# Moving the first weight pairs of the mLSTM merge behind the attention projection's last split, and its form loads behind the weight loads

## The chip, the cores and the metric

One core of a Trainium2 chip runs the whole program. The metric is the time of one execution on the device in microseconds (us), given as the median of several runs; lower is better. Beside the runs there is one profiled execution, whose trace is read below. Engine names are those of the profile: PE (TensorE matmuls), PEld (its weight loads), DVE (VectorE), ACT (ScalarE), POOL (GpSimd), SP (SyncE, which only issues DMAs here).

## The reference

One step of a hybrid decoder layer on 512 prompt tokens and 8 x 4 sample tokens, 544 columns in all, width 2048. An input projection feeds an mLSTM branch and a sliding-window attention branch. What matters here is the end of it:

```
y = (sigmoid(g_m) * einsum('btc,cd->btd', br_m, w_proj_m)
     + sigmoid(g_a) * einsum('btc,cd->btd', br_a, w_proj_a))
out = einsum('btc,cd->btd', y, w_out)
return _layernorm(DN_ALPHA * x + out, ln_w, ln_b)
```

The three matrices are 2048 x 2048, all data float32.

## The kernel before

Every large product is split into high and low parts. A weight block of 128 columns is loaded in two halves of 8 x 128 rows ("raw", 512 KB each, `load_half`, L205). `split` makes `wh` on ACT (a cast, L212) and then `wl = raw - wh` on DVE (L213). PE multiplies wh by the high and the low activation and wl by the high one. There are three buffers for raw halves loaded by L205, two for each of wh and wl, and so a split for the next product waits on PE releasing the one before the last.

Three stages meet at the place of the change.

1. **The attention projection** (`wa_`, 16 column blocks, `ct` 0 to 15, in `gemm`, matmuls at L229). Each block takes two halves; its two PSUM banks are multiplied into a tile `c5` on DVE (L1559) and stored (`d_t`, L1560).
2. Beside the last blocks, `first_forms` reads quarters of the mLSTM branch (`d_brm`, L1445), makes the forms f11, f1, f2, f12 (high and low) and stores two more forms to DRAM (`d_n3` at L1469, `d_s4` at L1479). The tiles for this come from a pool `fr` of four buffers.
3. **The merge** (`paired`, eight pairs of blocks of `w_proj_m`, matmuls at L634 for wh and L636 for wl). A pair is a seven-product scheme of the Strassen kind: seven half products, called steps 0 to 6 here, each 24 matmuls, instead of eight. Their weights are b11, b12 (raw, L205), b21, b22 (raw2, L605) and sums: step 1 takes `t1 = b11 + b12` and step 2 `b11 = t1 + b22`, both DVE additions at L614; two more sums are accumulating DMAs issued by POOL (L612). `prepare` emits the sums and the split up to two steps ahead, with a raised priority. The activations of the steps are the forms f11, f1, f2, f12, f3, f4, f22 in this order.

The first call of the generator `beside_merge` reads f3 back from `d_n3` (four DMAs into `fr`, `chunks_of`, `fetched`), then f4 from `d_s4` (four more, which wait for the f3 tiles to be free) and f22 into `room` (one 1088 KB DMA, L1501), and splits them (ACT L1492, DVE L1493). Steps 4, 5 and 6 need them. Gathering of the banks is done by `gather` (L644 to L663).

After the merge the output product begins in `first_two` (L1729), which splits four halves of `w_out`; just ahead of it the last columns of y are cast (`hilo`, ACT L265, DVE L266).

The order of instructions on each engine is worked out when the program is built, by a list scheduler with priorities: `tc.high_priority(offset=...)` raises what is emitted in it, `behind(...)` (`tc.issue_after`) keeps what is emitted in it behind a named earlier instruction in that order; neither adds a wait on the chip. PE's order in the merge is that of the code (`manual_schedule`). On the chip each of ACT, DVE, POOL and SP then takes its instructions in this order.

Of the kernel before, what the change touches and what calls it, by code (L numbers as in the profile page):

```python
# [5 lines left out]

# [1 line left out]

# [1 line left out]

# [68 lines left out]
def _build(tc, nc, i, o, es):  # L81
# [41 lines left out]
    def nm(s):  # L123
        count[0] += 1
        return f"{s}_{count[0]}"
# [7 lines left out]
    def r32(ap):  # L133
        return ap.bitcast(F32)
# [13 lines left out]
    state = {}  # L148
# [53 lines left out]

    def load_half(wv, c0, half):
        raw = wr.tile([128, 8, 128], F32, tag="raw", name=nm("raw"))
        state["load"] = nc.sync.dma_start(raw[:], wv[:, half * 8:half * 8 + 8, c0:c0 + 128])  # L205
        return raw

    def split(raw, p=None, tags=("wh", "wl")):
        p = p or wp
        wh = p.tile([128, 8, 128], F32R, tag=tags[0], name=nm("wh"))  # L210
        wl = p.tile([128, 8, 128], F32R, tag=tags[1], name=nm("wl"))
        state["wh"] = A.copy(wh[:], raw[:])  # L212
        state["wl"] = V.tensor_tensor(out=wl[:], in0=raw[:], in1=r32(wh[:]), op=ALU.subtract)  # L213
        return wh, wl

    @contextmanager
    def behind(*what):

        with ExitStack() as st:
            for w in what:  # L220
                st.enter_context(tc.issue_after(state[w].ins))
            yield
# [376 lines left out]
    def load_a(w):  # L599
        w["b11"], w["b12"] = (load_half(w["wv"], c0, 0) for c0 in (w["cA"], w["cB"]))  # L600

    def load_b(w):
        for n, c0 in (("b22", w["cB"]), ("b21", w["cA"])):
            w[n] = raw2()
            state["load"] = nc.sync.dma_start(w[n][:], w["wv"][:, 8:16, c0:c0 + 128])  # L605

    def prepare(w, n):


        def add(out, a, b):  # L610
            if w.get("acc") and out == a and n != 2:
                G.dma_start(out=w[out][:], in_=w[b][:], accum_op=ALU.add)  # L612
            else:
                V.tensor_tensor(out=w[out][:], in0=w[a][:], in1=w[b][:], op=ALU.add)  # L614
        if n == 1:
            w["t1"] = raw2()
            add("t1", "b11", "b12")
        elif n == 2:
            add("b11", "t1", "b22")
        w["hl", n] = split(w[("b11", "t1", "b11", "b21", "b12", "b22", "b21")[n]])  # L620
        if n == (1 if w.get("acc") else 3):
            add("b12", "b12", "b22")
        elif n == (3 if w.get("acc") else 4):
            add("b21", "b21", "b11")
# [40 lines left out]
    AHEAD = 400  # L665

    def paired(work, first=iter(()), early=False):

        steps = [(w, n) for w in work for n in range(7)]
        ready = 0  # L670
        load_a(work[0])
        load_b(work[0])
        for at, (w, n) in enumerate(steps):

            while ready < min(at + 3, len(steps)):
                with tc.high_priority(offset=AHEAD):
                    prepare(*steps[ready])
                ready += 1
            if early and at == 0:
                next(first)  # L680
            p = at // 7 + 1
            if n == 4 and "fetch" in w:
                w["fetch"]()
            if p < len(work):
                if n == 3:
                    load_a(work[p])
                elif n == 4:
                    load_b(work[p])
            half_product(w, n)
            with tc.high_priority(offset=AHEAD):  # L690
                gather(w, n)
            next(first, None)
            if n == 6:
                w["end"](w["O1"], w["O2"])
            tick()
# [741 lines left out]
    def fr():  # L1437
        return late["fr"].tile([128, 2, HT], F32, tag="fr", name=nm("fr"))

    def fetched(srcs, own=None):  # L1440
        out = []
        with behind("load"):
            for src in srcs:
                st = fr() if out or own is None else own
                nc.sync.dma_start(st[:], src.rearrange("k p t -> p k t"))  # L1445
                out.append(st[:] if st is not own else own)
        return out
# [47 lines left out]
    def beside_merge(f3, f4, f22, room):  # L1495

        split_form(f3, chunks_of(d_n3), -1.0)
        raws = chunks_of(d_s4)
        stage = room[0][:].rearrange("p a (b t) -> p (a b) t", b=2)
        with behind("load"):  # L1500
            nc.sync.dma_start(stage, d_brm[8:16, :, HT:T].rearrange("k p t -> p k t"))  # L1501
        yield
        yield
        split_form(f4, raws)
        for n in range(4):
            if n < 3:
                yield
            split_form(f22, [stage[:, n * 2:n * 2 + 2]], at=n)
        for _ in range(44):
            yield  # L1510

        def ask(ct, eng):
            late[ct] = c5t()[:]
            eng.dma_start(late[ct], d_y[ct])

        for ct in range(2):
            ask(ct, nc.sync)
        yield
        for ct in range(0, 14, 2):
            if ct % 4 == 0:  # L1520
                yh_.append(act3.tile([128, 4, T], F32R, tag="act", name=nm("yh")))
                yl_.append(act3.tile([128, 4, T], F32R, tag="act", name=nm("yl")))
            with behind("wh", "wl"):
                for c in (ct, ct + 1):
                    hilo(late[c], yh_[-1][:, c % 4], yl_[-1][:, c % 4])
                    if c < 4:
                        ask(c + 2, nc.gpsimd)
            yield
# [48 lines left out]
    wo_raw = [load_half(wo, 0, 0), load_half(wo, 128, 0), load_half(wo, 0, 1)]  # L1577
# [135 lines left out]
    def first_two():  # L1713

        both = [mm(True), mm(True)]
        for half in range(2):
            ws = []
            for ct in range(2):
                ws.append(split(wo_raw[half * 2 + ct]))
                if half == 0 and ct == 1:  # L1720
                    wo_raw.append(load_half(wo, 128, 1))
                    load_rows(0)
            for k0 in (0, 4):
                for ps, (wh, wl) in zip(both, ws):
                    for kk in range(k0, k0 + 4):
                        k = half * 8 + kk
                        for n, (a, b) in enumerate(((wh, yh), (wh, yl), (wl, yh))):
                            for f, c, w in CUT:
                                PE.matmul(ps[ALL, f, 0:w], a[:, kk], b(k, c, w),  # L1729
                                          start=(k == 0 and n == 0), stop=(k == 15 and n == 2))  # L1730
        return both
# [19 lines left out]
    for g in range(G3):  # L1751
        ct = 16 - G3 + g
        ps = sm()
        for half in range(2):
            raw = load_half(wo, ct * 128, half)
            if g < 2:
                wh, wl = (w[:, :, g] for w in w2[half])
                hilo(raw[:], wh, wl)
            else:
                w1.append(split(raw))  # L1760
                wh, wl = w1[half]
# [41 lines left out]
```

## Time and profile before

| | |
|---|---|
| median of 3 runs | 2522.78 us (2520.69 to 2524.19) |
| the profiled execution's own time | 2525.29 us |
| its span, first to last instruction | 2523.5 us |
| mean granted TensorE clock | 0.993 |
| PE busy / PEld busy | 2479.2 us (98%) / 2416.3 us (96%) |
| DVE / ACT / POOL busy | 1779.1 (71%) / 1212.5 (48%) / 366.8 (15%) us |
| attention projection's last half, start of merge, end of merge | 2114.6, 2130.7, 2300.3 us from the span's start |

How to read the rows below: the timeline gives start and duration of an instruction (or of equal ones that follow each other, xcount) and in square brackets the idle time of its engine just before it and what ended that. The table by stretches gives, for each stretch, its length and for each engine its busy time and number of instructions, then the mean granted clock (PEclk), the DMA engines' busy share and GB/s. The chain is the work that ended last, followed back from the program's end.

### The profile page before, as it was taken

The page shows a single profiled execution, that of the slowest core. Times are in us where ns is not written, and L with a number is a line of the kernel's source. Part 1 is how long each engine was busy: PE and PEld are TensorE (multiplying, and loading weights), DVE is VectorE, ACT ScalarE, POOL GpSimd, SP SyncE. Part 2 cuts the span into 40 slices and gives each one's busy share as a digit, 9 for nine tenths or more (in the row PEclk, how much of TensorE's full clock was granted, in tenths as well). Part 3 has the DMA queues.
Part 4 walks back from the last instruction along what each step waited for, and adds up shares of the span by engine and source line. Part 5 has one row for each costly group of instructions (what it writes and reads, how often), then busy time and mean ns, then how long its engine had stood idle before and what let it go on. Part 6 is the DMA issues. An engine that isn't in the chain of part 4 may idle for free.

```text
span 2523.5 us, 48930 instructions
## 1 busy us (share of the span) xinstructions
PE 2479.2 (98%) x19803; PEld 2416.3 (96%) x19803; DVE 1779.1 (71%) x2614; ACT 1212.5 (48%) x1971; POOL 366.8 (15%) x442
## 2 busy tenths in 40 slices
PE   8999999999999999999999999999999998999997
PEld 7999999999999999998999999999999998999997
DVE  7867777777677687588787888877765655776336
ACT  4447667667667665443433444344633323434221
POOL 2111111111111120131111121200000011110002
PEclk9999999999999999999999999999999999999998
DMA  6566666666666655478586775884645567988332
GB/s 192 136 167 149 162 152 154 157 152 154 158 151 154 157 123 146 105 231 249 161 260 197 223 232 146 254 246 127 190 160 165 165 206 201 254 208 240 101 98 82
DMA packets 548323, 439.20 MB, mean 174 GB/s; under 512 B 44256, under 2 KB 459280, under 8 KB 547808
## 3 DMA queue, kind: packets, MB, share of 16 engines
q1 hardware_dynamic: 535392, 389.85, 52.6%
q0 software_dynamic: 12704, 46.21, 10.0%
q8 instruction: 156, 2.56, 0.4%
q14 instruction: 71, 0.58, 0.1%
HBM read 302.68 MB, written 90.32 MB: 156 GB/s over the span
## 4 chain that ended last, share of the span: by engine, by line
PE 88%; DMA 3%; DVE 3%; issue 1%; ACT 1%; SPq 0%; POOL 0%; DVEq 0%; ACTq 0%
PE bank L634 42%; PE bank L636 21%; PE bank L229 11%; PE sm L1319 2%; PE sum L1130 1%; PE sm L1351 1%; PE sm L1364 1%; PE sm L744 1%; PE sm L784 1%; PE sm L774 1%; PE bank L1729 1%; PE sm L229 1%; DVE wl L213 1%; DMA d_n<-fr 1%; PE sm L1135 1%
## 5 line engine op out<-in xcount | busy, mean ns | idle before, releaser
L212 ACT CAST wh<-raw 128x1024 fp32r<-128x1024 f32 x628 | 657.7, 1048 | 887.5 <-PE bank L634 589.0
L213 DVE TENSOR_TENSOR wl<-raw,wh 128x1024 fp32r<-128x1024 f32 x628 | 780.4, 1244 | 296.6 <-ACT wh L212 295.1
L614 DVE TENSOR_TENSOR raw<-raw,raw 128x1024 f32<-128x1024 f32 x234 | 297.1, 1270 | 31.5 <-DMA raw<-in_w_proj_m 18.8
L634 PE MATMUL bank<-xk,wh 128*128 128x272 f32 x2304 | 315.8, 289 | 1.6 <-DVE ev L659 1.6
L634 PEld LDWEIGHTS bank<-xk,wh 128*128 128x128 f32 x2304 | 297.8, 188 | 4.5 <-ACT wh L212 1.8
L653 POOL TENSOR_TENSOR ev<-p,ev 128x272 f32<-128x272 f32 x80 | 113.7, 1422 | 564.5 <-ACT ev L652 527.6
L636 PE MATMUL bank<-xk,wl 128*128 128x272 f32 x1152 | 167.1, 287 | 0.0
L636 PEld LDWEIGHTS bank<-xk,wl 128*128 128x128 f32 x1152 | 153.5, 188 | 0.0
L634 PE MATMUL bank<-n2h,wh 128*128 128x272 f32 x576 | 147.4, 289 | 2.0 <-ACT wh L212 2.0
L634 PE MATMUL bank<-a11h,wh 128*128 128x272 f32 x576 | 148.8, 290 | 0.0
L634 PE MATMUL bank<-s4h,wh 128*128 128x272 f32 x576 | 148.6, 291 | 0.0
L634 PE MATMUL bank<-s1h,wh 128*128 128x272 f32 x576 | 148.6, 291 | 0.1
L634 PE MATMUL bank<-a11l,wh 128*128 128x272 f32 x576 | 147.8, 289 | 0.0
L634 PE MATMUL bank<-n3h,wh 128*128 128x272 f32 x576 | 147.5, 289 | 0.0
L634 PE MATMUL bank<-n3l,wh 128*128 128x272 f32 x576 | 146.9, 288 | 0.0
L634 PE MATMUL bank<-s4l,wh 128*128 128x272 f32 x576 | 146.7, 287 | 0.0
L634 PE MATMUL bank<-n2l,wh 128*128 128x272 f32 x576 | 146.6, 287 | 0.0
L634 PE MATMUL bank<-s1l,wh 128*128 128x272 f32 x576 | 146.6, 287 | 0.0
L612 POOL DMA_DIRECT2D raw<-raw x86 | 74.5, 867 | 407.6 <-DVE raw L614 173.7
L659 DVE SCALAR_TENSOR_TENSOR ev<-bank,ev 128x272 f32<-128x272 f32 x80 | 35.3, 442 | 120.1 <-PE bank L636 118.3
L229 PE MATMUL bank<-bh,wl 128*128 128x272 f32 x512 | 110.1, 292 | 7.9 <-DVE wl L213 7.9
L634 PEld LDWEIGHTS bank<-n2h,wh 128*128 128x128 f32 x576 | 108.2, 188 | 3.2 <-ACT wh L212 2.2
(503 smaller groups left out, 5953.4 us busy)
## 6 DMA issues: line engine op xcount, KB each, us to landing
raw<-in_w_in SPq DMA_DIRECT2D x296, 512.0 KB
raw<-raw POOLq DMA_DIRECT2D x86, 512.0 KB, 4.9
C<-in_state_mlstm_C SPq DMA_DIRECT2D x32, 1024.0 KB
out<-C SPq DMA_DIRECT2D x64, 512.0 KB
raw<-in_w_proj_a SPq DMA_DIRECT2D x32, 512.0 KB
raw<-in_w_proj_m SPq DMA_DIRECT2D x32, 512.0 KB
raw<-in_w_out SPq DMA_DIRECT2D x32, 512.0 KB
d_sgm<-ev SPq DMA_DIRECT2D x16, 272.0 KB
```

The lines of the kernel that those rows point to most:

```text
L212: state["wh"] = A.copy(wh[:], raw[:])
L213: state["wl"] = V.tensor_tensor(out=wl[:], in0=raw[:], in1=r32(wh[:]), op=ALU.subtract)
L229: PE.matmul(ps[ALL, f, 0:w], a[:, kk], b(k, c, w), start=(k == 0 and n == 0), stop=(k == 15 and n == 2))
L612: G.dma_start(out=w[out][:], in_=w[b][:], accum_op=ALU.add)
L614: V.tensor_tensor(out=w[out][:], in0=w[a][:], in1=w[b][:], op=ALU.add)
L634: PE.matmul(ps, wh[:, k], x(p, k), start=(first and k == 0 and p == 0), stop=False, skip_group_check=True)
L636: PE.matmul(ps, wl[:, k], x(0, k), start=False, stop=(k == 7), skip_group_check=True)
L653: G.tensor_tensor(out=c22, in0=p1, in1=c11, op=ALU.subtract)
L659: V.scalar_tensor_tensor(c22, B0, -sc, c22, op0=ALU.mult, op1=ALU.add)
L744: PE.matmul(pp[:, c0 + w0:c0 + 256], qs[a][:, j * 128:j * 128 + 128], kx[:, k0:k0 + 256 - w0], start=(n == 0), stop=(n == 1))
L774: PE.transpose(pt[:, (m - m0_) * 128:(m - m0_) * 128 + 128], s_[:, b, 128:256] if own else s_[:, b + 1, 0:128], ident)
L1319: PE.matmul(pp[:, 0:258], a[:, b * 128:b * 128 + 128], b_[:, b, f], start=(b == 0 and n == 0), stop=(b == 3 and n == 2))
```

## The change

Three things are altered.

- In the merge's step 0, everything that `prepare` emits for steps 0, 1 and 2 is kept behind the newest `wh` and `wl` split: the first of these are those of the attention projection's last half, the later ones those of the step before.
- The reads of `fetched` and of `room` are kept behind the newest load of either kind: `state["raw"]` is now the newest `load_half`, `state["load"]` remains the newest load of any weight (raw or raw2).
- In `first_two` the splits of the first half of `w_out` get a raised priority.

```diff
     def load_half(wv, c0, half):
...
-        state["load"] = nc.sync.dma_start(raw[:], wv[:, half * 8:half * 8 + 8, c0:c0 + 128])
+        state["load"] = state["raw"] = nc.sync.dma_start(raw[:], wv[:, half * 8:half * 8 + 8, c0:c0 + 128])
...
             while ready < min(at + 3, len(steps)):
-                with tc.high_priority(offset=AHEAD):
+                with tc.high_priority(offset=AHEAD), (behind("wh", "wl") if early and at == 0 else nullcontext()):
                     prepare(*steps[ready])
...
     def fetched(srcs, own=None):
         out = []
-        with behind("load"):
+        with behind("load", "raw"):
...
         stage = room[0][:].rearrange("p a (b t) -> p (a b) t", b=2)
-        with behind("load"):
+        with behind("load", "raw"):
             nc.sync.dma_start(stage, d_brm[8:16, :, HT:T].rearrange("k p t -> p k t"))
...
             for ct in range(2):
-                ws.append(split(wo_raw[half * 2 + ct]))
+                with tc.high_priority(offset=AHEAD if half == 0 else 0):
+                    ws.append(split(wo_raw[half * 2 + ct]))
```

What this does to the engines' order, at the three places where it matters. First DVE, at the seam from the attention projection to the merge. The sum into `raw2_3391_25193` is t1 (of b11 `raw_3385_25181` and b12 `raw_3386_25183`); `wl_3376_25117` is the last half of the attention projection, `wl_3390_25190` step 0, `wl_3393_25196` step 1; `c5_3359` and `c5_3368` are the results of blocks 14 and 15:

```order
-L614 TENSOR_TENSOR raw2_3391_25193<-raw_3385_25181,raw_3386_25183 128x1024
 L1559 TENSOR_TENSOR c5_3359_24927<-bank_3360_24929,c5_3359_24927 128x272
 L1559 TENSOR_TENSOR c5_3359_24927<-bank_3361_24930,c5_3359_24927 128x272
 L213 TENSOR_TENSOR wl_3376_25117<-raw_3374_25114,wh_3375_25116 128x1024
 L213 TENSOR_TENSOR wl_3390_25190<-raw_3385_25181,wh_3389_25189 128x1024
-L614 TENSOR_TENSOR raw_3385_25181<-raw2_3391_25193,raw2_3387_25185 128x1024
+L614 TENSOR_TENSOR raw2_3391_25193<-raw_3385_25181,raw_3386_25183 128x1024
 L1559 TENSOR_TENSOR c5_3368_25056<-bank_3369_25058,c5_3368_25056 128x272
 L1559 TENSOR_TENSOR c5_3368_25056<-bank_3370_25059,c5_3368_25056 128x272
 L213 TENSOR_TENSOR wl_3393_25196<-raw2_3391_25193,wh_3392_25195 128x1024
+L614 TENSOR_TENSOR raw_3385_25181<-raw2_3391_25193,raw2_3387_25185 128x1024
 L213 TENSOR_TENSOR wl_3395_25202<-raw_3385_25181,wh_3394_25201 128x1024
```

The t1 sum has moved from ahead of block 14's results and two splits to behind them, and the step 2 sum from ahead of block 15's results to behind step 1's split. On ACT, step 0's gather (L644, which reads the bank of step 0) has moved from behind the four f3 casts to ahead of step 2's cast `wh_3394`.

Second SP, at the same place; `raw_3374` is the attention projection's last half, `raw_3385` b11, `raw_3386` b12, and the four `fr<-d_n3` are the reads of f3. Before:

```order
L1445 DMA fr_3397_25207<-d_n3_109 128x2x272
L1445 DMA fr_3398_25209<-d_n3_109 128x2x272
L1560 DMA d_t_107<-c5_3346_24790 128x544
L205 DMA raw_3385_25181<-in_w_proj_m 128x8x128
L1554 DMA c5_3368_25056<-d_sga_106 128x544
L1479 DMA d_s4_110<-fr_3358_24908 128x2x272
L1445 DMA fr_3399_25211<-d_n3_109 128x2x272
L205 DMA raw_3386_25183<-in_w_proj_m 128x8x128
```

And now SP reads, from the same store on:

```order
L1560 DMA d_t_107<-c5_3346_24790 128x544
L205 DMA raw_3385_25181<-in_w_proj_m 128x8x128
L1554 DMA c5_3368_25056<-d_sga_106 128x544
L1479 DMA d_s4_110<-fr_3358_24908 128x2x272
L205 DMA raw_3386_25183<-in_w_proj_m 128x8x128
L1445 DMA fr_3396_25205<-d_n3_109 128x2x272
L1445 DMA fr_3397_25207<-d_n3_109 128x2x272
L1445 DMA fr_3398_25209<-d_n3_109 128x2x272
L1445 DMA fr_3399_25211<-d_n3_109 128x2x272
```

The load of b12 has moved ahead of all four reads of f3; three of them stood ahead of b11's load or between the loads.

Third DVE, some 20 us later, where f4 and f22 are split (`wl_3415` is step 5's split, L659 the gather of step 4):

```order
 L1493 SCALAR_TENSOR_TENSOR f4l_3380_25174<-fr_3400_25221,f4h_3379_25173 128x544
-L1493 SCALAR_TENSOR_TENSOR f22l_3382_25176<-room_3383_25177,f22h_3381_25175 128x544
+L213 TENSOR_TENSOR wl_3415_25332<-raw2_3387_25185,wh_3414_25331 128x1024
+L1493 SCALAR_TENSOR_TENSOR f22l_3382_25176<-room_3383_25177,f22h_3381_25175 128x544 x2
 L1493 SCALAR_TENSOR_TENSOR f4l_3380_25174<-fr_3401_25223,f4h_3379_25173 128x544
+L659 SCALAR_TENSOR_TENSOR ev_3410_25288<-bank_3413_25303,ev_3410_25288 128x272
 L1493 SCALAR_TENSOR_TENSOR f4l_3380_25174<-fr_3402_25225,f4h_3379_25173 128x544
-L213 TENSOR_TENSOR wl_3415_25332<-raw2_3387_25185,wh_3414_25331 128x1024
-L1493 SCALAR_TENSOR_TENSOR f22l_3382_25176<-room_3383_25177,f22h_3381_25175 128x544
 L1493 SCALAR_TENSOR_TENSOR f4l_3380_25174<-fr_3403_25227,f4h_3379_25173 128x544
-L659 SCALAR_TENSOR_TENSOR ev_3410_25288<-bank_3413_25303,ev_3410_25288 128x272
```

Step 5's split now follows the first chunk of f4 at once, on ACT as well as on DVE, and step 4's gather stands ahead of the last two chunks of f4 instead of behind them.

At the output the order of ACT and DVE is unaltered up to the third column block: the casts of y stand ahead of the first splits of `w_out` as before. Only PE's order inside `first_two` differs, in which blocks of matmuls of the two columns alternate, with the same first six matmuls; and one load of `w_out` (`raw_3661`) stands ahead of the loads of `ln_w` and `ln_b` on SP, and its cast ahead of two evacuations on ACT.

More of the change, by code (lines that the diff above doesn't have):

```diff
@@ L9 @@
-from contextlib import ExitStack, contextmanager
+from contextlib import ExitStack, contextmanager, nullcontext
 import numpy as np
```

## The prediction

> **What bounds the kernel now.** I read the page's shares first, then PE's waits from 2080 us on, then the stretches and the timeline around the longest of them, and last the chain of waits back from it.
>
> ```profile
> PE 2479.2 (98%) x19803; PEld 2416.3 (96%) x19803; DVE 1779.1 (71%) x2614; ACT 1212.5 (48%) x1971; POOL 366.8 (15%) x442
> ...
> PE bank L229 <- DVE wl L213: 7.9, 1, 7.9
> PE bank L1729 <- ACT wh L212: 2.3, 2, 1.6
> PE bank L634 <- DVE f4l L1493: 0.4, 1, 0.4
> ```
>
> PE is busy for 98% of the span, so only its gaps can be won. From 2080 us on there are three kinds: one of 7.9 us at the seam of attention projection and merge, 2.3 us at the output's first splits, 0.4 us at f4. The change touches all three places.
>
> ```profile
> 2108.58:2114.60 6.02, 6.02 (x50) 6.02 (x49) 0.00 (x0) 1.05 (x2) 0.00 (x0) 1.00 0.83 248
> 2114.60:2122.89 8.29, 0.42 (x5) 0.20 (x3) 3.12 (x5) 0.75 (x1) 0.92 (x1) 0.68 0.39 111
> 2122.89:2130.70 7.81, 7.81 (x45) 7.81 (x45) 2.30 (x2) 0.05 (x1) 0.00 (x0) 0.68 0.75 155
> 2130.70:2133.71 3.01, 3.01 (x26) 3.01 (x25) 2.01 (x3) 1.75 (x2) 0.00 (x0) 1.00 0.25 93
> 2133.71:2145.75 12.04, 12.04 (x98) 12.04 (x97) 9.37 (x13) 8.65 (x15) 2.52 (x2) 1.00 1.02 298
> 2145.75:2149.46 3.71, 3.27 (x26) 3.05 (x25) 3.71 (x6) 3.55 (x7) 0.00 (x0) 1.00 0.91 279
> ...
> 2114.60 0.41 PE L229 MATMUL bank<-bl,wh 128*128 128x272 f32 x2
> 2122.89 0.82 PE L229 MATMUL bank<-bh,wl 128*128 128x272 f32 x2 [7.87 <-DVE wl L213]
> 2130.70 0.29 PE L634 MATMUL bank<-f11h,wh 128*128 128x272 f32 x1
> ```
>
> The first stretch is a whole half of the attention projection: 48 matmuls (8 blocks of rows, 3 products, 2 column ranges) in 6.02 us, 0.1254 us each at a clock of 1.00. The last half begins the same way, does two matmuls with wh at 2114.60 and then has no wl until 2122.89. The remaining matmuls take 7.81 us, since the granted clock over the gap and after it is 0.68. Step 0 of the merge begins at 2130.70; a step takes 3.01 us. DVE tells why wl is late:
>
> ```profile
> 2103.38 1.23 DVE L213 TENSOR_TENSOR wl<-raw,wh 128x1024 fp32r<-128x1024 f32 x1 [1.72 <-ACT wh L212]
> 2119.77 1.23 DVE L614 TENSOR_TENSOR raw<-raw,raw 128x1024 f32<-128x1024 f32 x1 [15.17 <-DMA raw<-in_w_proj_m]
> 2120.92 0.78 DVE L1559 TENSOR_TENSOR c<-bank,c 128x272 f32<-128x272 f32 x2
> 2121.61 2.35 DVE L213 TENSOR_TENSOR wl<-raw,wh 128x1024 fp32r<-128x1024 f32 x2
> ...
> 2108.28 1.05 ACT L212 CAST wh<-raw 128x1024 fp32r<-128x1024 f32 x1 [4.93 <-PE bank L229]
> 2114.30 1.05 ACT L212 CAST wh<-raw 128x1024 fp32r<-128x1024 f32 x1 [4.97 <-PE bank L229]
> 2130.65 1.05 ACT L212 CAST wh<-raw 128x1024 fp32r<-128x1024 f32 x1 [15.30 <-PE bank L229]
> ```
>
> DVE stood idle for 15.17 us in front of the t1 sum (L614), which waited for the load of b12. The wl that PE needed is the first of the two in the 2121.61 row; its cast had been ready since 2108.28 + 1.05. It stood behind a sum for step 1, which nobody needed yet. Why b12 came so late is in the chain:
>
> ```profile
> 2107.09 3.42 DMA d_t<-c
> 2110.94 4.04 DMA d_s<-fr
> 2115.41 4.27 DMA raw<-in_w_proj_m
> ...
> 2098.24 0.78 DVE L1559 TENSOR_TENSOR c<-bank,c 128x272 f32<-128x272 f32 x2
> 2101.10 1.77 POOL L1478 TENSOR_TENSOR fr<-fr,ev 128x544 f32<-128x544 f32 x1 [3.99 <-DVE f12l L266]
> ```
>
> SP issued b12's load only at 2115.41, behind a read of f3 that waited for the buffer of a store (4.04 us), which stood behind a load of c5 that waited for the store of another c5 (3.42 us).
>
> **Term 1, the gap at the seam.** The t1 sum moves behind the wl of the last half. That wl then has ahead of it on DVE the wl of 2103.38 and block 14's two results (0.78 us), which need PE's end of block 14 at 2108.58. It runs from about 2109.4 to 2110.7, some 4 us before PE wants it. PE goes on at 2114.60 + 2 x 0.1254 = 2114.85 and does its 46 matmuls in 5.77 us: step 0 begins at 2120.62 instead of 2130.70. The saving is 10.08 us, of which 8.04 is waiting and 2.04 slow matmuls. Step 0's own split needs the cast at 2114.30 and a wl of 1.2 us, so it is ready at 2116.6.
>
> The Trainium skill (TensorE: Matmul & The Clock Gate, Part 1: The HAM clock gate) says that the array falls to half rate after an idle window of about 3.4 us and comes back after one of work. By that figure the slow part would be worth about 1.7 us, an estimate, and the term 9.7; the row's 7.81 us decides.
>
> **Term 2, steps 1 and 2, and the loads.** Moved past on SP are the four reads of f3. b12's load now needs the raw buffer whose wl ends at 2104.61. Ahead of it on SP are the c5 load, whose buffer is free once a result of 2099.02 is stored (3.42 us, so 2102.4), and the d_s4 store, ready when POOL ends at 2102.87. So it is issued near 2104.6 at best and at 2115.41 at worst, landing between 2108.9 and 2119.7 (4.27 us). At the late end t1 would end at 2120.9 and step 1's cast at 2122.0, still ahead of step 1 at 2120.62 + 3.01 = 2123.63; so the term is nothing between both ends. What hides it is step 0. If b12 landed after about 2121, PE would wait for step 1 one for one. The early end is nearer, since its waits are those that the rows show. POOL's accumulation of b22 on b12, queued behind t1, moves with it and has until step 4.
>
> **Term 3, f3, f4 and f22 against steps 4 to 6.** Here the cover is thin, because the seam's pause hid work that now has to fit behind PE. Times below are counted from the start of step 0.
>
> ```profile
> 2132.96 1.05 ACT L212 CAST wh<-raw 128x1024 fp32r<-128x1024 f32 x1 [1.26 <-DVE wl L213]
> 2133.91 2.30 ACT L1492 ACTIVATE f3h<-fr 128x544 fp32r<-128x544 f32 x4
> 2142.16 0.66 ACT L1492 ACTIVATE f4h<-fr 128x544 fp32r<-128x544 f32 x1 [2.18 <-DMA fr<-d_s]
> 2144.36 1.03 ACT L212 CAST wh<-raw 128x1024 fp32r<-128x1024 f32 x1
> 2146.95 1.05 ACT L212 CAST wh<-raw 128x1024 fp32r<-128x1024 f32 x1 [0.16 <-DMA raw<-raw]
> 2155.67 0.40 ACT L644 ACTIVATE p<-bank 128x272 f32<-128x272 f32 x1 [2.69 <-PE bank L636]
> ...
> 2135.18 2.62 DVE L1493 SCALAR_TENSOR_TENSOR f3l<-fr,f3h 128x544 fp32r<-128x544 f32 x4
> 2147.21 0.72 DVE L1493 SCALAR_TENSOR_TENSOR f4l<-fr,f4h 128x544 fp32r<-128x544 f32 x1
> 2147.84 0.43 DVE L659 SCALAR_TENSOR_TENSOR ev<-bank,ev 128x272 f32<-128x272 f32 x1
> 2152.46 0.28 PE L634 MATMUL bank<-f11h,wh 128*128 128x272 f32 x1
> 2139.53 0.86 POOL L612 DMA_DIRECT2D raw<-raw  x1
> ...
> 2135.93 6.21 DMA fr<-d_s
> ```
>
> Step 2's cast came at +2.26 (2132.96) and now stands behind step 0's gather, which by the second pair runs at +3.21 (2155.67 against its step 0 at 2152.46). So it starts at about +3.55: 1.3 us later. It is used at +6.02, so PE does not see this. The f3 splits behind it slip by the same 1.3 us and end near +8.4, wanted at +12.04: hidden. But each f4 read waits for an f3 buffer, and is issued at +6.5 instead of +5.2 (2135.93). There the price is open: f4 landed 6.21 us after issue, in a stretch in which the DMA engines were full (share 1.02, 298 GB/s) with b22 of the next pair (512 KB) and f22's 1088 KB issued ahead. If it is the bytes ahead that set the landing, f4 comes at +11.46 as before; if the read takes 6.21 us from its issue, 1.3 us later. A still earlier landing would win: step 5 took 3.71 us, 0.70 over a step, and that is the most to be had. I take the unchanged landing, because the full DMA row is the row of this very place.
>
> The Trainium skill (DMA: Bandwidth & Descriptors, Queues, rings and completion order) has descriptors consumed in ring order on each DMA engine. By it reads behind f22's bytes wait for them whenever they are issued, and the sum stays at 9.4; without it the sum is 8.1. The trace shows no single read's start, so no row here settles it.
>
> After f4's first cast at +11.46 the order has changed: step 5's cast (1.03) and wl come at once, so DVE idles some 0.3 us for that cast where it did f22 before, and L659 (0.43, about 0.35 of DVE's queue) now stands ahead of the last two f4 chunks. So f4's last chunk, done 5.77 us after that first cast (2147.93), is done 6.4 after it. PE waits 0.65 us more in step 5: a loss of 0.65. Step 6 then starts at about +19.4. Its cast waits for a POOL accumulation (issued at 2139.53, landed at 2146.95, which is +16.25); if that slips by the 1.3 us as well, the cast is done by +18.6: hidden with 0.8 us left.
>
> **Term 4, the output.** The casts of y and the first splits keep their order on ACT and DVE, so the 2.3 us gap should stay. PE's reordered blocks use the same operands, all there by 2306.4. The load moved ahead of `ln_w` wins nothing where PE has no gap. Cost and gain: nothing, with up to 0.7 us either way if a first matmul of the second column finds its operand differently:
>
> ```profile
> 2301.89 0.52 PE L1729 MATMUL bank<-yh,wh 128*128 128x256 f32 x2 [1.61 <-ACT wh L212]
> 2303.38 0.39 PE L1729 MATMUL bank<-yh,wh 128*128 128x256 f32 x1 [0.73 <-ACT wh L212]
> 2305.18 1.22 DVE L213 TENSOR_TENSOR wl<-raw,wh 128x1024 fp32r<-128x1024 f32 x1
> ```
>
> **The sum.** 10.08 - 0.65 = 9.4 us. The profiled execution took 2525.29 us (span 2523.5 and 1.8 around it), 2.5 above the median of the runs, 0.1%; the saving is taken as the same for both. So 2515.9 for such an execution and 2522.78 - 9.4 = 2513.4 for the median.
>
> **The rivals.**
>
> - *f4 slips with its issue.* Nothing changes but the landing, +1.3: 8.1 us won, 2514.7. For it: f4's issue does hang on f3. Against it: the full DMA engines.
> - *The wait moves to step 1.* b12's load gets ahead of f3's reads, but SP is one queue and the c5 load and d_s4 store stay ahead of it. If they held it until it landed at 2125, PE would wait 4 to 5 us at step 1: 5 won, 2517.8. Against it: neither had to wait past 2103 for its own data.
> - *The gain goes elsewhere, no change.* The eased seam only lets PE run ahead to f3 and f4, whose stores and reads keep their old clock times. f4's first cast at 2142.16 would then be +21.5, and PE would wait 10 us at step 5: step 6 starts where it did, some 2523. For it: the stores of d_s4 and the SP queue are what the chain goes through. Against it: the f4 reads wait for f3's buffers, f3's casts for PE's release of weight buffers (15.30 us of wait in the 2130.65 row), and those come 10 us earlier.
> - *Slower.* The same place with the reads of f4 crowded by the loads that the earlier start brings forward: f4's cast beyond +21 costs more than the seam gives, beyond +26 it is 0.2% slower. At +27.5 the wait is 16 us longer and, with a second slow stretch of 2.04 us, 2531 results. It would take a read of 20 us in place of 6.21; 298 GB/s of 1.02 share leave no row for that.
>
> **Chances.** The forecast 0.62 (own range 2511.5 to 2514.5 with f4's 0.7 and the output's 0.7), f4 slipping 0.19, the wait at step 1 0.06, no change 0.09, slower 0.04. About 0.2% (5 us) is what a measurement of this kernel can tell from no change, so the first two and most of the third are faster: 0.86; same 0.10; slower 0.04. The range runs from 2510.5 (all of step 5's excess won as well, and the runs' own spread of 2 us below) to 2517.8 (the wait at step 1).
>
> **What would show it.** In the changed kernel's profile PE's 7.9 us wait at L229 is gone and no clock under 1.00 stands around 2115 to 2130; the t1 sum runs between two splits with an idle time before it that holds nobody; step 0 starts near 2120.6. PE waits for f4l about 1.0 to 1.1 us (0.44 before), and the 2.3 us at L1729 stand. I am wrong if PE has a new wait of over 3 us in steps 1 to 6, or if f4's first cast lies later than 13 us after step 0.

## The result and the profile after

The changed kernel takes 2519.05 us in the median of 20 runs (2512.77 to 2523.63); the kernel before takes 2523.76 us beside it, also of 20 (2520.69 to 2530.96). By medians that is 4.7 us less; the ratio over the runs is 0.9972 with a 95% interval of 0.9964 to 0.9981, so 7.1 us of 2523.8 (4.8 to 9.1). It is faster, by 0.3%. The profiled execution took 2515.00 us (span 2513.2).

PE's waits from 2080 us on in the changed kernel (us in total, times, longest):

```profile
PE bank L1730 <- ACT wh L212: 2.0, 2, 1.3
PE bank L634 <- DVE f4l L1493: 1.3, 2, 1.1
PE bank L634 <- ACT f4h L1492: 0.4, 1, 0.4
```

The 7.9 us at L229 are gone, the output's wait stands (its line is now L1730), and the waits at f4 have grown from 0.4 to 1.7 us. PE is busy for 2479.0 us, 99% of the span. The stretches tell more. The first runs from the cast of the attention projection's last half to step 0, the second over steps 0 to 4, the next two over step 5 and the start of step 6, the last is the output's first 12 us:

```profile
2104.09:2116.19 12.10, 12.10 (x98) 12.10 (x97) 4.37 (x5) 2.11 (x3) 0.92 (x1) 1.00 0.61 183
2116.19:2131.24 15.05, 15.05 (x122) 15.05 (x121) 11.48 (x14) 9.15 (x14) 1.72 (x2) 1.00 0.93 259
2131.24:2135.40 4.16, 2.46 (x15) 1.73 (x13) 4.16 (x8) 3.93 (x8) 0.00 (x0) 1.00 1.07 298
2135.40:2139.00 3.60, 3.60 (x18) 3.60 (x17) 3.60 (x5) 1.62 (x3) 0.00 (x0) 0.53 1.15 318
...
2288.75:2300.75 12.00, 9.97 (x65) 9.56 (x64) 9.26 (x14) 4.21 (x6) 0.00 (x0) 0.86 0.53 171
```

The seam is a full 12.10 us of PE at a clock of 1.00. But right behind the waits in step 5 stand 3.60 us at a clock of 0.53, in which 18 matmuls ran, and at the output the clock over 12 us is 0.86. The same stretch of the output in the kernel before had it at 1.00:

```profile
2300.11:2312.11 12.00, 9.66 (x75) 9.25 (x74) 9.56 (x15) 4.53 (x8) 0.00 (x0) 1.00 0.52 167
```

The seam itself, in the changed kernel on DVE and SP:

```profile
2105.17 1.23 DVE L213 TENSOR_TENSOR wl<-raw,wh 128x1024 fp32r<-128x1024 f32 x1 [0.17 <-ACT wh L212]
2111.20 1.23 DVE L213 TENSOR_TENSOR wl<-raw,wh 128x1024 fp32r<-128x1024 f32 x1 [4.80 <-ACT wh L212]
2112.34 1.22 DVE L614 TENSOR_TENSOR raw<-raw,raw 128x1024 f32<-128x1024 f32 x1
2118.41 1.22 DVE L614 TENSOR_TENSOR raw<-raw,raw 128x1024 f32<-128x1024 f32 x1
...
2100.44 0.37 SPq L205 DMA_DIRECT2D raw<-in_w_proj_m  x1
2100.86 2.81 SPq L1445 DMA_DIRECT2D fr<-d_n  x4
```

The last half's wl runs as soon as its cast is done. The t1 sum (L614 at 2112.34) comes behind step 0's wl and waits for nothing; the sum for step 2 (2118.41) is no longer ahead of block 15's results. That t1 finds its data is because b12's load was issued at 2100.44, ahead of all reads of f3.

The two profiles can't be compared by their spans, because work that the change doesn't touch came 4.2 us earlier in the second by chance: the cast of the attention projection's last half (ACT L212) ran at 2108.28 before and at 2104.09 after. So here is each profile from that cast to the end of the span, for the seven further kernels below as well (one profiled execution each; pair 1 is steps 0 to 6 of the first pair of the merge):

| kernel | cast to step 0 | pair 1 | rest of merge, and output | cast to end | median of runs, ratio to before [95%] |
|---|---|---|---|---|---|
| before | 22.42 | 21.76 | 371.04 | 415.2 | |
| after | 12.10 | 25.24 | 371.77 | 409.1 | 2519.05, 0.9972 [0.9964, 0.9981] |
| c_only | 21.45 | 22.23 | 371.34 | 415.0 | 2528.71, 1.001 [0.9998, 1.0021] |
| a_only | 12.10 | 24.40 | 373.26 | 409.8 | 2519.27, 0.9982 [0.9971, 0.9993] |
| b_only | 12.10 | 22.07 | 371.34 | 405.5 | 2513.48, 0.9954 [0.9941, 0.9967] |
| a_two | 12.10 | 22.19 | 371.88 | 406.2 | 2516.21, 0.9974 [0.9964, 0.9984] |
| f4_first | 12.10 | 26.08 | 370.04 | 408.2 | 2520.23, 0.9979 [0.9969, 0.9989] |
| out_first | 12.10 | 25.32 | 367.65 | 405.1 | 2512.76, 0.9957 [0.9943, 0.9971] |
| b_out | 12.10 | 21.73 | 368.63 | 402.5 | 2513.15, 0.9956 [0.9938, 0.9973] |

From the cast on the change saves 6.1 us: 10.32 won at the seam, 3.48 lost in pair 1, 0.73 lost in the rest. The kernel before ran beside them with medians of 2525.09 (23 runs, for a_only, b_only, f4_first and out_first) and 2523.73 (23 runs, for a_two, b_out and c_only).

### The profile page after: what moved, and what is told of

It reads as the page before. It is cut to its first block, busy times and chain, and to the rows that moved or that the text cites. A ratio compares the mean times of both kernels' runs of the same rounds, so it can differ in the third digit from the quotient of the medians.

```text
span 2513.2 us, 48929 instructions
## 1 busy us (share of the span) xinstructions
PE 2479.0 (99%) x19803; PEld 2416.6 (96%) x19803; DVE 1777.3 (71%) x2614; ACT 1211.7 (48%) x1971; POOL 366.2 (15%) x442
## 4 chain that ended last, share of the span: by engine, by line
PE 91%; DVE 2%; DMA 1%; issue 1%; ACT 1%; DVEq 0%; SPq 0%; ACTq 0%; POOLq 0%
PE bank L634 43%; PE bank L636 21%; PE bank L229 13%; PE sm L1319 2%; PE sum L1130 1%; PE sm L1351 1%; PE sm L1364 1%; PE sm L744 1%; PE sm L784 1%; PE bank L1730 1%; PE sm L774 1%; PE sm L229 1%; DMA raw<-in_w_in 1%; PE sm L1135 1%; DVE z L1679 0%
## 5 line engine op out<-in xcount | busy, mean ns | idle before, releaser
L212 ACT CAST wh<-raw 128x1024 fp32r<-128x1024 f32 x628 | 657.7, 1048 | 878.7 <-PE bank L634 606.9
L614 DVE TENSOR_TENSOR raw<-raw,raw 128x1024 f32<-128x1024 f32 x234 | 296.8, 1268 | 14.2 <-DMA raw<-in_w_in 7.3
L659 DVE SCALAR_TENSOR_TENSOR ev<-bank,ev 128x272 f32<-128x272 f32 x80 | 35.3, 441 | 120.1 <-PE bank L636 118.3
L634 PEld LDWEIGHTS bank<-s4h,wh 128*128 128x128 f32 x576 | 108.3, 188 | 1.5 <-issue 1.2
```

Of the source, the lines that this page charges most:

```text
L634: PE.matmul(ps, wh[:, k], x(p, k), start=(first and k == 0 and p == 0), stop=False, skip_group_check=True)
L659: V.scalar_tensor_tensor(c22, B0, -sc, c22, op0=ALU.mult, op1=ALU.add)
```

## The experiments

The change has three parts: A, what `prepare` emits in step 0 kept behind the splits; B, the form loads behind the newest load of either kind; C, the raised priority at the output. In the order in which each engine takes its instructions, A alone moves rows of DVE and ACT at the seam and, further on, of SP and (inside `first_two`) of PE; B alone moves only rows on SP; C moves none.

**a_only: A without B and C.**

```
             while ready < min(at + 3, len(steps)):
-                with tc.high_priority(offset=AHEAD):
+                with tc.high_priority(offset=AHEAD), (behind("wh", "wl") if early and at == 0 else nullcontext()):
                     prepare(*steps[ready])
```

> Only the sums and splits of steps 0 to 2 are kept behind the last split; the form loads stay where they were, so SP issues b12's load behind the read of f3 as before. Theory 1 (the gap was DVE's order alone): the 7.9 us wait at L229 is gone, b12 still lands about 9 us after step 0's predecessor half began but t1 has until step 1, so PE waits 0 to 0.5 us at step 1; f4 behaves as in the changed kernel (first cast near +12.6 us from step 0, pair 1 lasting 24 to 25 us against 21.8); time as the changed kernel's, ratio to before 0.997. Rival (b12's late load is the cause, DVE's order only where it showed): PE waits 4 to 8 us at step 1 instead and the ratio is 0.999 to 1.001.

Measured: 2519.27 us, ratio 0.9982 (0.9971 to 0.9993). The seam's gap is gone, pair 1 takes 24.40 us. PE's waits, and f4's first cast (step 0 began at 2119.84):

```profile
PE bank L1729 <- ACT wh L212: 2.4, 2, 1.7
PE bank L634 <- DVE f4l L1493: 1.3, 2, 1.1
PE bank L634 <- ACT f4h L1492: 0.9, 1, 0.9
...
2133.32 0.66 ACT L1492 ACTIVATE f4h<-fr 128x544 fp32r<-128x544 f32 x1 [4.20 <-DMA fr<-d_s]
```

A alone heals the seam, and no wait at step 1 takes the gap's place, which was the rival. A alone also brings the waits at f4: 2.2 us of them. f4's first cast is 13.48 us after step 0, later than the +12.6 that was expected. Here the clock over pair 1 stayed at 1.00, so the pair lost less than in the changed kernel in spite of longer waits; at the output it fell instead (0.72 over the first 12 us), and the rest is 2.2 us longer than before.

**b_only: B without A and C.**

```
-        state["load"] = nc.sync.dma_start(...)
+        state["load"] = state["raw"] = nc.sync.dma_start(...)
...
-        with behind("load"):
+        with behind("load", "raw"):
```

> Only the form loads are kept behind the newest raw load; DVE, ACT and PE keep the order of before. Theory 1 (order on DVE must change): t1 still stands ahead of the last wl, so part of the 7.9 us wait stays. Theory 2 (either cure is enough): b12's load is issued about 11 us earlier, t1 runs some 5 us before PE wants the last wl, the gap is gone too; and since step 0's gather stays behind the f3 casts, f4 is read at +5.2 us and cast first at +11.5, so pair 1 lasts 21.8 us as before and PE's wait for f4 stays near 0.4 us. Then this kernel is some 3 us faster than the changed one, 10 us under before: ratio 0.996. If f4's later landing in the changed kernel comes from the loads and not from the gather's place, pair 1 lasts 24 to 25 us here as well and the ratio is 0.997.

Measured: 2513.48 us, ratio 0.9954 (0.9941 to 0.9967), below the interval of A alone. DVE at the seam, and the waits of PE:

```profile
2115.55 1.23 DVE L614 TENSOR_TENSOR raw<-raw,raw 128x1024 f32<-128x1024 f32 x1 [6.24 <-DMA raw<-in_w_proj_m]
...
2117.39 1.22 DVE L213 TENSOR_TENSOR wl<-raw,wh 128x1024 fp32r<-128x1024 f32 x1
...
PE bank L634 <- DVE f4l L1493: 0.6, 1, 0.6
PE bank L229 <- DVE wl L213: 0.5, 1, 0.5
```

The t1 sum still stands ahead of the wl that PE needs, and DVE still waits for b12 there, but only until 2115.55: the wl is done at 2118.61, some 0.7 us before PE begins its products with it (step 0 begins at 2125.09, the half 6.02 earlier, and two matmuls of 0.125 come first: 2119.32). So no part of the seam's wait is left (the 0.5 us at L229 lie at 2329.72, in the output), and the theory that either cure is enough holds. Each part alone removes the whole gap; they don't add. And since B moves nothing on DVE and ACT, pair 1 stays at 22.07 us.

**a_two: the change, but with the sum for step 2 not held back.** If A's cost in pair 1 comes from one row, it is that sum: it reads t1's buffer, and behind step 1's split it ends 1.2 us later. The next b22 goes into that buffer, and SP has f22's 1088 KB and the reads of f4 behind b22's load.

```
-                with tc.high_priority(offset=AHEAD), (behind("wh", "wl") if early and at == 0 else nullcontext()):
+                with tc.high_priority(offset=AHEAD), (behind("wh", "wl") if early and at == 0 and ready < 2 else nullcontext()):
```

> The changed kernel with one thing of it taken back: what step 0 prepares for steps 0 and 1 (the t1 sum among it) stays behind the splits, the sum for step 2 does not. On every engine but SP the only instruction that stands elsewhere than before the change is t1; SP loads b12 ahead of f3's reads, as in the change. Theory (the lengthening of pair 1 comes from the step 2 sum, which frees t1's buffer 1.2 us later, so that the load of the next b22, f22's 1088 KB and the reads of f4 behind them all slip): the seam's 7.9 us stay won, f4's first cast is at +11.5 to +11.8 after step 0 (+12.78 in the changed kernel, +11.75 where only the loads were moved), PE waits 0.4 to 0.6 us for f4l, pair 1 takes 21.8 to 22.1 us (25.24 in the changed kernel, 22.07 where only the loads were moved) at a clock of 1.00. Median about 2513.5, ratio 0.9955. Rival (the earlier start of step 0 itself crowds f4's reads, whatever the step 2 sum does): pair 1 stays at 24.4 to 25.3 us and f4's first cast beyond +12.5; median about 2518 to 2519, ratio 0.9975. Rival 2 (the sum for step 1 behind the splits costs as much as it wins): step 1 waits, pair 1 above 23.

Measured: 2516.21 us, ratio 0.9974 (0.9964 to 0.9984). PE waits 0.6 us for f4l, as the theory said. Pair 1 takes 22.19 us and f4's first cast is at +11.88, each just outside the theory's range (22.1 and +11.8) and far from the 25.24 and +12.78 of the changed kernel. SP, for the kernel before (step 0 at 2130.70), the changed one (2116.19) and this one (2118.63), the load of f22 and the reads of f4 in each (the load of b22 stands 0.43 to 0.47 us ahead of f22's):

```profile
2133.41 0.57 SPq L1501 DMA_DIRECT2D room<-d_brm  x1
2135.93 2.27 SPq L1445 DMA_DIRECT2D fr<-d_s  x4
```

```profile
2120.15 0.53 SPq L1501 DMA_DIRECT2D room<-d_brm  x1
2122.68 2.27 SPq L1445 DMA_DIRECT2D fr<-d_s  x4
```

```profile
2121.43 0.53 SPq L1501 DMA_DIRECT2D room<-d_brm  x1
2123.86 2.27 SPq L1445 DMA_DIRECT2D fr<-d_s  x4
```

Counted from step 0, f22's load is issued at +2.71, +3.96 and +2.80, and f4's reads at +5.23, +6.49 and +5.23. All of them slip together by about 1.25 us in the changed kernel and come back with this one edit. What b22's load (L605) waited for on SP is in the traces, first before, then in the changed kernel:

```profile
SPq L605 <- DVE wl L213: 1.0, 1, 1.0
```

```profile
SPq L605 <- DVE raw L614: 2.2, 1, 2.2
```

Before, and again in a_two, the last reader of t1's buffer is step 1's split; in the changed kernel, and in a_only (2.4 us), it is the moved sum. The reads of f4 wait for f3's splits (f3l) in all of these kernels. The median of the runs alone doesn't decide between theory and rival (0.9974 is the rival's number, 0.9955 the theory's); the profile does, and the spread of the runs, shown below, is why. The edit also puts step 0's gather on ACT back behind the casts of f3; the split of step 2, and f3's splits behind it, follow both the sum and the gather, so which of the two rows carries more of f4's slip was not tried apart.

**f4_first: the change, with f22's load put behind the reads of f4 on SP.**

```
-                nc.sync.dma_start(st[:], src.rearrange("k p t -> p k t"))
+                state["f4"] = nc.sync.dma_start(st[:], src.rearrange("k p t -> p k t"))
...
-        with behind("load", "raw"):
+        with behind("load", "raw", "f4"):
             nc.sync.dma_start(stage, d_brm[8:16, :, HT:T].rearrange("k p t -> p k t"))
```

> The changed kernel, with f22's 1088 KB load issued behind the four reads of f4 instead of ahead of them. If bytes ahead on the DMA engines set f4's landing (6.2 us from issue in both kernels): the reads land in 3 to 4 us, f4's first cast comes near +9.5 to +10 instead of +12.6, PE's 1.7 us of waits in step 5 and the slow clock behind them are gone, pair 1 lasts 21.2 to 22 us instead of 25.1, ratio to before 0.996. If the read simply takes 6.2 us: first cast at +12.5, pair 1 some 24 us, less what the new order on DVE gives (about 0.6).

Measured: 2520.23 us, ratio 0.9979 (0.9969 to 0.9989): no gain over the change, and pair 1 takes 26.08 us where 21.2 to 22 were expected. SP, ACT and PE at the place (step 0 at 2126.88):

```profile
2133.37 2.64 SPq L1445 DMA_DIRECT2D fr<-d_s  x4
2136.11 0.42 SPq L1501 DMA_DIRECT2D room<-d_brm  x1
...
2136.30 0.66 ACT L1492 ACTIVATE f4h<-fr 128x544 fp32r<-128x544 f32 x1
2146.11 1.20 ACT L1492 ACTIVATE f22h<-room 128x544 fp32r<-128x544 f32 x2 [5.20 <-DMA room<-d_brm]
2148.29 0.60 PE L634 MATMUL bank<-f22h,wh 128*128 128x272 f32 x1 [3.20 <-ACT wh L212]
...
2136.11 9.98 DMA room<-d_brm
```

The reads of f4 are issued at +6.49 as in the changed kernel, but the first cast runs at +9.42, at most 2.9 us after the issue, where it took 6.26 behind f22's load. The issue is as late and the landing 3.36 us sooner, so it is the bytes ahead that set most of f4's landing. The waits at f4 are gone, and PE waits 3.2 us in step 6 instead: f22 now lands 9.98 us after its issue, and step 6's cast of wh stands behind f22's casts on ACT. With the sum moved, one of f4 and f22 is late in both orders of their loads. The Trainium skill (DMA: Bandwidth & Descriptors, Queues, rings and completion order) says that each DMA engine takes descriptors in ring order; the 6.26 and 2.9 us agree with it.

**c_only: C alone.**

```
-                ws.append(split(wo_raw[half * 2 + ct]))
+                with tc.high_priority(offset=AHEAD if half == 0 else 0):
+                    ws.append(split(wo_raw[half * 2 + ct]))
```

> Only the raised priority of the first two output splits. Every engine's instructions stand in the order of the kernel before, so theory and rival agree on no change: ratio 1.000 with an interval that holds 1, seam wait 7 to 8 us, output wait 2.3 us. It shows how large a difference the runs' own spread makes between two equal programs. If the ratio lies beyond 0.999 or 1.001, the intervals of the other runs have to be read with that much more doubt.

The built program is indeed that of the kernel before, instruction for instruction, and the changed kernel without C is likewise the changed kernel; PE's other order inside `first_two` comes from A. So C does nothing, and this run measures one program twice. Measured: 2528.71 us, ratio 1.001 (0.9998 to 1.0021). Its profile has 7.7 us of seam wait, 1.7 us at the output, and 415.0 us from the cast to the end, 0.2 less than before. Yet its median is 5.0 us above that of before, and its ratio stands at the 1.001 beyond which its expectation called for doubt: differences of 0.1% between the kernels here settle nothing, and the change's 0.3% is some three times as much. One source of such a spread lies far ahead of the change. The same 60 us in three kernels, before, after and c_only (PE's busy time and number of matmuls, then PEld, DVE, ACT, POOL, the granted clock, DMA share, GB/s):

```profile
1000.00:1060.00 60.00, 60.00 (x478) 56.56 (x477) 35.23 (x49) 21.05 (x32) 9.95 (x15) 0.97 0.42 106
```

```profile
1000.00:1060.00 60.00, 60.00 (x490) 56.70 (x488) 35.80 (x48) 22.04 (x33) 9.88 (x15) 1.00 0.43 111
```

```profile
1000.00:1060.00 60.00, 60.00 (x419) 56.30 (x418) 30.24 (x43) 18.33 (x28) 4.87 (x5) 0.83 0.30 76
```

In b_out it is 419 matmuls and 0.83, too. PE counts as busy throughout, and yet 59 to 71 matmuls fewer get done in c_only and b_out than in the other two, 7 to 9 us at 0.12 to 0.13 us each. Within one kernel it comes and goes as well: b_only's profiled execution, with a clock of 0.75 from 1020 to 1040 us, took 2520.38 us, its other four runs 2512.53 to 2514.49. A median of 5 to 20 such runs carries an error of some microseconds; in their profiles before and c_only agree within 1.0 us in each part and 0.2 in the sum.

**out_first: the change, with the casts of y's columns 8 to 13 put behind the first two splits of `w_out`.** The kernel's order has them ahead, on ACT and DVE alike.

```
-                for c in (ct, ct + 1):
+                for c in (ct, ct + 1) if ct < 8 else ():
...
+    ws0 = [split(wo_raw[ct]) for ct in range(2)]
+    with behind("wh", "wl"):
+        for ct in range(8, 14):
+            hilo(late[ct], yh_[ct // 4][:, ct % 4], yl_[ct // 4][:, ct % 4])
...
-                with tc.high_priority(offset=AHEAD if half == 0 else 0):
-                    ws.append(split(wo_raw[half * 2 + ct]))
+                ws.append(ws0[ct] if half == 0 else split(wo_raw[half * 2 + ct]))
```

> The changed kernel, with y's columns 8 to 13 cast behind the first two splits of w_out instead of ahead of them, which the change's third part did not bring about (ACT's and DVE's order there was as before). If the casts ahead of the splits are why PE waits at the output: the 2.0 us of waits at the output's first splits fall to under 0.5, and the slow clock that followed them in the changed kernel's profile (0.79 over 2289 to 2295) does not come; 2 to 3.5 us from the merge's last matmul to the end. If the splits wait for something else (the load of w_out, the buffer): the wait stays at 2.

Measured: 2512.76 us, ratio 0.9957 (0.9943 to 0.9971). ACT's casts at the output, first in the changed kernel, then here, and the first 12 us of the output here:

```profile
2285.84 3.39 ACT L265 CAST yh<-room 128x544 fp32r<-128x544 f32 x6
2289.13 1.05 ACT L212 CAST wh<-raw 128x1024 fp32r<-128x1024 f32 x1
```

```profile
2285.59 1.04 ACT L212 CAST wh<-raw 128x1024 fp32r<-128x1024 f32 x1
...
2288.54 3.38 ACT L265 CAST yh<-room 128x544 fp32r<-128x544 f32 x6
...
2288.38:2300.38 12.00, 12.00 (x98) 12.00 (x97) 10.61 (x16) 5.89 (x10) 0.00 (x0) 1.00 0.58 178
```

Six casts of y, 3.39 us, were what made the first split of `w_out` late. With them behind, PE does 98 matmuls in the 12 us instead of 65, and the stretch from pair 2 to the end is 4.1 us shorter, where 2 to 3.5 were expected: 2.0 of wait, and of the rest the larger part the clock that doesn't fall. That is what the words of part C intend, and what C doesn't do.

**b_out: B alone, with the output as in out_first.**

> Only the form loads behind the raw loads (the part of the change that moves nothing but SP's rows), and at the output the casts of y's last six columns put behind the first two splits of w_out. Theory (the two gains add): seam 0 to 0.5 us of waiting, pair 1 22.1 us, no wait at the output's start (1.8 us and 2.4 us of first-block delay where only the loads were moved). From the last half of the attention projection to the end 405.45 less 1.8 to 2.5 us: 403 to 403.7 us (409.1 in the changed kernel). Median 2510 to 2512, ratio 0.994 to 0.995, the fastest of all. Rival (a wait at the output costs nothing in the runs without a profile, since the 2.0 us of it are covered by the splits that then run ahead): as with the loads alone, 2513.5 and 0.9954.

Measured: 2513.15 us, ratio 0.9956 (0.9938 to 0.9973), runs from 2507.39 to 2520.00. From the cast to the end it takes 402.5 us, 0.5 below the range expected and the shortest of all: 12.7 less than before, 6.7 less than the changed kernel. PE's waits from 2080 us on are down to these:

```profile
PE bank L636 <- DVE wl L213: 0.6, 1, 0.6
PE bank L634 <- DVE f4l L1493: 0.4, 1, 0.4
```

By the runs' ratio the two gains don't add (0.9954 for the loads alone, 0.9956 here, the intervals overlapping nearly whole), so that the expected 2510 to 2512 us was missed; by the profile they do (405.5 to 402.5). The runs differ in their mean granted clock: b_out's three at 0.995 and 0.996 took 2507.39 to 2510.12 us, its three at 0.991 and 0.992 took 2516.18 to 2520.00. Among the runs at 0.994 or more, out_first has four from 2510.43 to 2513.02 and b_only four from 2512.53 to 2514.49, so there the gains add; but these few runs were picked out afterwards. The lowest run of all kernels, 2507.39 us, is of this one. That it is faster than the kernel before is shown; that it beats b_only or out_first is not settled by these runs.

## Why the prediction came out as it did

**Right: term 1.** The gap and its slow matmuls were put at 10.08 us; from the last half's cast to step 0 it is 22.42 - 12.10 = 10.32. b12's load was expected about 3.7 us ahead of the last half's cast (2104.6 against 2108.28) if nothing but the c5 load and the store were ahead of it: it was issued 3.65 us ahead (2100.44 against 2104.09). Term 2 therefore holds too: t1 ended at 2113.56, and PE waits for nothing from step 0 to step 4 (15.05 us in the row).

**Mis-sized: term 3.** It took 0.65 us off; pair 1 lost 3.48. The step that failed is "if it is the bytes ahead that set the landing, f4 comes at +11.46 as before". The bytes ahead do set it (f4_first), but they were held where they had been, at +2.7, and they slip as well, since b22's load waits for the buffer of t1, which the moved sum of step 2 now frees 1.2 us later. The sum was read only for what it delivers (step 2's weights, in time), not for the buffer that it gives back:

```profile
2128.97 0.66 ACT L1492 ACTIVATE f4h<-fr 128x544 fp32r<-128x544 f32 x1 [3.50 <-DMA fr<-d_s]
...
2132.27 0.39 PE L634 MATMUL bank<-f4h,wh 128*128 128x272 f32 x1 [0.37 <-ACT f4h L1492]
2133.78 0.39 PE L634 MATMUL bank<-f4l,wh 128*128 128x272 f32 x1 [1.12 <-DVE f4l L1493]
2134.77 0.39 PE L634 MATMUL bank<-f4l,wh 128*128 128x272 f32 x1 [0.21 <-DVE f4l L1493]
...
2138.06 0.43 PE L634 MATMUL bank<-f22h,wh 128*128 128x272 f32 x1
2138.29 0.43 PE L634 MATMUL bank<-f22l,wh 128*128 128x272 f32 x1
```

f4's first cast is 12.78 us after step 0, 1.32 later: the rival "f4 slips with its issue" has the right number. The reads of f4 did slip as forecast, but in f4_first they are issued as late and land 3.36 us sooner, which speaks for the bytes and against the issue alone. PE waits 1.70 us instead of 0.44. That is 1.26 of the 3.48; the other 2.2 no case held. Most of it are matmuls 0.23 us apart instead of 0.125 in the 3.60 us after the waits (1.7 us, an estimate from the clock: 3.6 x 0.47). About 0.5 is in the starts around the waits, three here and one before, which lie 0.16 to 0.37 us further apart at each than its idle time explains.

**Mis-sized: term 4.** The gap stands as forecast, 2.0 us against 2.3, and so do its causes on ACT. But the clock fell behind it (0.86), and the output is 1.1 us longer (224.45 against 223.39 from the merge's end), beyond the 0.7 allowed.

**The whole.** 10.32 - 3.48 - 0.73 = 6.1 us by the profiles and 7.1 by the ratio, where 9.4 had been forecast. The ratio on the 2522.78 us shown gives 2515.7, inside the range; the median of the 20 runs, 2519.05, is 1.3 us above its upper end, and half of what the stretch at 1000 us can cost is more than that. That the ratio's figure still lies in the range is luck in part: the upper end was set for a wait at step 1, which did not come, and 3.3 us were lost in other places. Of the two signs of error that had been named neither came: no new wait over 3 us, and f4's first cast at 12.78, not beyond 13. Both were set too wide to see a loss of 3.5 us.

## What to carry to other kernels

When an instruction is moved back, ask not only who waits for its result but who waits for the buffers that it reads: a load, and all that stands behind that load in its queue, may hang on them. Where a gap comes from an operand that lands late, moving the load ahead in its queue (b_only) disturbed less here than moving the consumer (a_only), and doing both paid the consumer's price for nothing. Compare profiles from the last mark that the change can't touch; between spans, chance ahead of the change (4.2 us) was here not much smaller than the effect (6.1).

## What the runs showed of the hardware

Short waits, none of them near the seam's 7.87 us, can halve the clock, and don't always. Behind 1.70 us of waits in three pieces (after, step 5) and behind about 2.0 us at the output (after; 1.7 in a_two) 3.60 us ran at 0.53 and the 12 us at 0.86, behind 2.4 us (a_only, output) the 12 us at 0.72; behind 2.2 us (a_only, step 5), 2.3 us (before, output), 1.8 us (b_only, output) and 1.7 us (c_only, output) the clock stayed at 1.00. What decides is in the clock's records. In all nine profiles every stretch at 0.50 lasts 3.41 us or a multiple of it (but for the last, which the trace's end cuts off), and its ends lie on a grid of 3.41 us that runs through the whole profile, in another place in each. What counts is how much of a wait falls into one window of this grid. First the changed kernel's window with step 5's waits, then the two of a_only:

```profile
2132.01:2135.43 3.42, 1.83 (x10) 1.32 (x10) 3.42 (x7) 3.19 (x7) 0.00 (x0) 1.00 1.13 329
```

```profile
2133.72:2137.14 3.42, 2.42 (x16) 1.84 (x14) 2.91 (x4) 3.42 (x7) 0.00 (x0) 1.00 1.06 256
2137.14:2140.55 3.41, 2.19 (x14) 1.89 (x15) 3.41 (x6) 3.07 (x6) 0.00 (x0) 1.00 1.08 305
```

In the first PE is busy for 1.83 us, and the next window, 2135.43 to 2138.84, is the one at 0.50. In a_only longer waits are parted between two windows, with 2.42 and 2.19 us busy, and the clock stays. From 2080 us on, the nine profiles have 14 windows at a clock of 1.00 in which PE is busy for a share of 0.50 or less: the next is at 0.50 each time. Behind none with a share of 0.64 or more does the clock fall, and of four between (0.53 to 0.59) three are followed by 0.50. So whether a wait of about 2 us halves the clock hangs on where the grid falls. The Trainium skill (TensorE: Matmul & The Clock Gate, Part 1: The HAM clock gate) has the activity window free-running, so that the point of a change depends on where in the window the work falls; that waits of equal length go both ways agrees with it, and the grid of 3.41 us shows such a window.

More costly was a stretch in which PE never waits. Between 1007 and 1050 us four groups of 32 narrow matmuls (32 elements a row, 16 each at L943 and L944) stand between the matmuls of weight steps. Here are those at L943 in two windows of the grid that follow each other (PE's and PEld's busy time and instructions, the clock, DMA share, GB/s), first in c_only, then in the changed kernel:

```profile
1018.30:1021.71 3.41, 1.70 (x12) 1.15 (x12) 1.00 0.00 0
1021.71:1025.12 3.41, 0.95 (x6) 0.57 (x4) 0.50 0.47 122
```

```profile
1015.85:1019.26 3.41, 1.19 (x8) 0.76 (x8) 1.00 0.04 13
1019.26:1022.67 3.41, 1.23 (x9) 0.76 (x8) 1.00 0.20 38
```

In c_only most of the group falls into one window, and the next is at 0.50; in the changed kernel the group is parted about evenly, and the clock stays. That holds for all 36 groups of the nine profiles: 17 have 22 to 30 of their 32 starts in one window, and the next is at 0.50 each time; the other 19 have at most 18 in any window, and the clock never falls behind them. At full clock the groups follow each other by 10.26 us, almost three windows, so that a program which parts the first group parts all four.

The granted clock there went between 0.50 and 1.00 in c_only, f4_first, b_out and b_only, fell once for 3.41 us in before and a_two, and stayed at 1.00 in after, a_only and out_first, with the same instructions in the same order. It is worth up to some 8 us, more than the change. No kernel here moved or widened the narrow matmuls, so why a group within one window lowers the clock stays open.
